# Row sums of 16,384 rows of 1,024: one row per partition moved from the blocks to the tail

## The chip, the cores and the metric

The kernel runs on one core of a Trainium2 chip. The metric is the device time of one execution in microseconds (us). Three runs of the kernel before took 160.62, 160.66 and 160.67 us; their median is 160.66.

## The reference

`x` has the shape 32 x 512 x 1024 in float32, so 16,384 rows of 1,024 numbers (4 KB each, 67.1 MB in all). Each row is summed, and the sum is multiplied by 0.5:

```python
def reference(x: np.ndarray, multiplier: float) -> np.ndarray:
    return (np.sum(x, axis=-1) * multiplier).astype(np.float32)
```

The result has 16,384 numbers, 64 KB.

## The kernel before

The rows are dealt out to the 128 partitions of the on-chip memory, 128 rows to each, in three groups (lines 39 to 50).

- The *blocks*: partition p owns `own` = 112 consecutive rows, rows 112p to 112p + 111 of the input. They are loaded in seven blocks of B = 16 rows per partition (64 KB per partition, 8 MB per block).
- The *tail*: after the 128 x 112 block rows come 128 x 15 rows, of which partition p owns `tail` = 15 consecutive ones. They are loaded last, in pieces of 7, 5 and 2 rows (`pieces`, line 157), and the 15th row in two cuts of 608 and 416 numbers into a tile of its own, `end` (lines 162 to 165).
- The *lead*: the last 128 rows of the input, one to a partition, loaded first (line 114).

So in the input a partition's block rows start 112 x 4 KB = 448 KB after those of the partition before, and its tail rows 15 x 4 KB = 60 KB after.

All DMAs are issued by SyncE (SP) on one queue, in the order of the program: the lead, blocks 0 to 6, the tail's five loads, and three stores. There are three buffers of 16 rows per partition, `buf`. Blocks 0, 1 and 2 find them free; their loads and the lead's are moved to the program's entry (lines 203 to 229) so that they start before anything else. The load of block b, from 3 on, waits until VectorE has summed block b - 3 (`freed`, line 122); the tail goes into block 4's buffer (line 156).

VectorE waits for each block and sums all its 16 rows with one `reduce_sum` (line 134), and scales the 16 sums into `res` with a small second instruction (line 140). Block 6, the last, is halved: VectorE takes 8 rows, and ScalarE takes the other 8, one instruction pair each (`act_row`, line 89, with the running sum written to a column of `res`). In the tail the rows are dealt by the set `on_act` (line 175): ScalarE takes rows 4, 5, 6, 10, 11 and 13, VectorE takes the others with `dve_sum` (line 98), which adds a row's two halves and sums them in one instruction. The 15th row is VectorE's: first the 608 numbers, then the 416 together with the first part's sum (lines 187 to 192).

Three stores follow on SP. The early store (line 167) writes the blocks' results, 112 numbers (448 B) per partition, and is issued when VectorE and ScalarE are done with block 6. The lead's store (line 171) writes 4 x 32 numbers. The last store (line 195) writes the tail's results, 15 numbers (60 B) per partition, and waits for both engines. The program ends when all three have landed.

Of the kernel before, what the change touches and what calls it, by code (L numbers as in the profile page):

```python
# [9 lines left out]
def kernel(  # L10
# [24 lines left out]
    rows = N // P  # L35
# [3 lines left out]
    B = 16  # L39
    n_blocks = rows // B  # L40
    assert N == P * rows and rows == n_blocks * B
    own = rows - B
    tail = B - 1
    lead0 = P * (own + tail)
    x_rows = x_flat[0 : P * own, :].rearrange("(p c) d -> p c d", p=P)
    x_last = x_flat[P * own : lead0, :].rearrange("(p c) d -> p c d", p=P)
# [27 lines left out]
    def marks(i, engine):  # L74

        s = dve_done if engine == "dve" else act_done
        i.then_inc(s, 1)
        counts[engine] += 1
        return counts[engine]

    def load(name, dst, src, free=None):
        landed = sem(name)
        i = nc.sync.dma_start(out=dst, in_=src)  # L83
        if free is not None:
            i.wait_op(dve_done, free, "sem-ge")
        i.then_inc(landed, 16)
        return landed

    def act_row(t, r, col):
        return nc.scalar.activation(  # L90
            out=t[:, r, :],
            in_=t[:, r, :],
            func=mybir.ActivationFunctionType.Copy,
            scale=mul,
            accum_out=res[:, col : col + 1],
        )

    def dve_sum(row, dst, scale):
        mid = row.shape[-1] // 2
        return nc.vector.tensor_tensor_reduce(  # L100
            out=row[:, 0:mid],
            in0=row[:, 0:mid],
            in1=row[:, mid:],
            scale=scale,
            scalar=0.0,
            op0=ADD,
            op1=ADD,
            accum_out=dst,
        )
# [3 lines left out]
    freed = []  # L113
    lead_landed = load("lead_landed", lead, x_lead)
    for b in range(n_blocks - 1):
        c0 = b * B
        t = buf[b % bufs]
        landed = load(
            f"landed{b}",
            t,  # L120
            x_rows[:, c0 : c0 + B, :],
            freed[b - bufs] if b >= bufs else None,
        )
        h = B if b < n_blocks - 2 else B // 2
        if b == 0:
            nc.vector.wait_ge(lead_landed, 16)
            nc.vector.wait_ge(dve_done, zeroed)
            summed = marks(dve_sum(lead, lead_sq[:, 0:1], mul), "dve")
            turned = nc.vector.transpose(out=lead_tr, in_=lead_sq)  # L129
            turned.wait_op(dve_done, summed, "sem-ge")  # L130
            marks(turned, "dve")
        nc.vector.wait_ge(landed, 16)
        done = marks(
            nc.vector.reduce_sum(  # L134
                out=sums[:, c0 : c0 + h], in_=t[:, 0:h, :], axis=mybir.AxisListType.X
            ),
            "dve",
        )
        freed.append(done)
        scaled = nc.vector.tensor_single_scalar(  # L140
            out=res[:, c0 : c0 + h],
            in_=sums[:, c0 : c0 + h],
            scalar=mul,
            op=mybir.AluOpType.mult,
        )
        scaled.wait_op(dve_done, done, "sem-ge")
        early_dve = marks(scaled, "dve")
        if h < B:
            nc.scalar.wait_ge(landed, 16)
            for r in range(h, B):  # L150
                i = act_row(t, r, c0 + r)
            early_act = marks(i, "act")

    c0 = (n_blocks - 1) * B
    t = buf[(n_blocks - 1) % bufs]
    nc.sync.wait_ge(dve_done, freed[n_blocks - 1 - bufs])
    pieces = [(0, 7), (7, 12), (12, 14)]
    landed = [
        load(f"landed_p{k}", t[:, lo:hi, :], x_last[:, lo:hi, :])
        for k, (lo, hi) in enumerate(pieces)  # L160
# [11 lines left out]
    lead_stored = sem("lead_stored")  # L172
    lead_store.then_inc(lead_stored, 16)

    on_act = {4, 5, 6, 10, 11, 13}
    for k, (lo, hi) in enumerate(pieces):
        on = [r for r in range(lo, hi) if r in on_act]
        nc.scalar.wait_ge(landed[k], 16)
# [86 lines left out]
```

## Time and profile before

| What | Value |
|---|---|
| Median of 3 runs | 160.66 us |
| The profiled execution | 160.62 us |
| Its span in the profile | 159.3 us |
| Read from the chip's memory (HBM), written to it | 67.11 MB, 0.07 MB |
| Mean rate over the span | 422 GB/s |
| VectorE (DVE) busy | 120.2 us, 75% |
| ScalarE (ACT) busy | 16.3 us, 10% |
| Share of the DMA queue's packets of 16 engines' span | 98.0% |

Times in the profile count from the span's start. DVE is VectorE, ACT is ScalarE, SPq is the sequencer of SyncE, which issues the DMAs. A name such as `sums<-xb` tells the tile written and the tile read, with buffer numbers left out; `L134` is line 134. A DMA is carried out by up to 16 DMA engines, and it has landed when all have counted up its semaphore; each load here gives every partition one packet, so each of the 16 engines has 8 of them.

### The profile page before, as it was taken

Reading aid. Unit: us, or ns where it says so; the run is one execution under the profiler, and the core shown is the slowest. Engines: PE = TensorE matmul, PEld = TensorE weight load, DVE = VectorE, ACT = ScalarE, POOL = GpSimd, SP = SyncE. Lnnn points to the kernel's source line nnn. Section 1 sums busy time; section 2 is a strip of 40 time slices with the busy share of each in tenths; the row PEclk is TensorE's granted clock in tenths of the full one; section 3 lists DMA queues with packets and bytes.
Section 4 is the critical chain, followed back from the end, with each engine's and each line's share of the span. In section 5 each row is a group of like instructions: output and inputs, shape, how many; then the busy total and the mean of one; then the engine's idle time right before and its main releaser. Section 6 shows DMA issues by size and latency. Waiting matters only on the chain.

```text
span 159.3 us, 128 instructions
## 1 busy us (share of the span) xinstructions
DVE 120.2 (75%) x39; ACT 16.3 (10%) x29; POOL 0.2 (0%) x4
## 2 busy tenths in 40 slices
DVE  2000029999499995999869997899959999599744
ACT  2000000000000000000000000000000000099844
POOL 0000000000000000000000000000000000000000
DMA  9969989899699699699699898996996996999994
GB/s 395 510 280 527 411 379 527 379 411 527 263 527 527 263 527 527 263 527 494 296 527 428 362 527 379 411 527 280 510 527 263 527 527 263 436 403 433 442 397 144
DMA packets 2168, 67.18 MB, mean 422 GB/s; under 512 B 504, under 2 KB 632, under 8 KB 888
## 3 DMA queue, kind: packets, MB, share of 16 engines
q1 hardware_dynamic: 2168, 67.18, 98.0%
HBM read 67.11 MB, written 0.07 MB: 422 GB/s over the span
## 4 chain that ended last, share of the span: by engine, by line
DMA 75%; DVE 22%; SPq 1%; issue 0%
DMA xb<-in_x_dram 52%; DMA end<-in_x_dram 24%; DVE sums L134 22%; SPq L83 1%; DVE end L100 1%; DVE res L140 0%; DVE res L100 0%
## 5 line engine op out<-in xcount | busy, mean ns | idle before, releaser
L134 DVE TENSOR_REDUCE sums<-xb 128x16 f32<-128x16384 f32 (+1 forms) x7 | 112.0, 16001 | 30.3 <-DMA xb<-in_x_dram 30.3
L90 ACT ACTIVATE xb<-xb 128x1024 f32<-128x1024 f32 x14 | 14.6, 1046 | 138.1 <-DMA xb<-in_x_dram 138.0
L100 DVE CUSTOM_DVE_ANT_0 xb<-xb 128x512 f32<-128x512 f32 x8 | 5.1, 689 | 3.9 <-DMA xb<-in_x_dram 3.9
L90 ACT ACTIVATION_READ_ACCUMULATOR xb<-xb 128x1 f32 x14 | 2.6, 188 | 0.0
L111 DVE MEMSET end<- 128x2 f32 x1 | 0.1, 60 | 2.9 <-PEq L26 2.9
L90 ACT ACT_TABLE_LOAD x1 | 1.3, 1283 | 2.9 <-PEq L26 2.9
L140 DVE TENSOR_SCALAR res<-sums 128x16 f32<-128x16 f32 (+1 forms) x7 | 1.2, 174 | 0.2
L100 DVE CUSTOM_DVE_ANT_0 end<-end 128x304 f32<-128x304 f32 (+1 forms) x2 | 0.9, 428 | 0.1
L100 DVE CUSTOM_DVE_ANT_0 lead<-lead 128x512 f32<-128x512 f32 x1 | 0.7, 693 | 0.2 <-DMA lead<-in_x_dram 0.2
L100 DVE DVE_READ_ACCUMULATOR2_ANT res<- 128x1 f32 x9 | 0.8, 83 | 0.0
L129 DVE STREAM_TRANSPOSE lead_tr<-lead_sq 128x32 f32<-128x32 f32 x1 | 0.2, 211 | 0.0
L246 POOL MEMSET const-bfloat16-1.0<- 128x1 bf16 x1 | 0.1, 101 | 0.0
L246 POOL MEMSET const-uint8-127<- 128x1 uint8 x1 | 0.1, 101 | 0.0
L246 POOL MEMSET const-float32-0.0<- 128x1 f32 x1 | 0.1, 98 | 0.2 <-issue 0.2
L246 POOL MEMSET const-float32-1.0<- 128x1 f32 x1 | 0.1, 98 | 0.0
L112 DVE MEMSET lead_sq<- 128x32 f32 x1 | 0.1, 85 | 0.0
L100 DVE DVE_READ_ACCUMULATOR2_ANT end<- 128x1 f32 x1 | 0.1, 84 | 0.0
L100 DVE DVE_READ_ACCUMULATOR2_ANT lead_sq<- 128x1 f32 x1 | 0.1, 83 | 0.0
## 6 DMA issues: line engine op xcount, KB each, us to landing
xb<-in_x_dram SPq DMA_DIRECT2D x1, 3584.0 KB, 29.9
xb<-in_x_dram SPq DMA_DIRECT2D x1, 2560.0 KB, 35.7
xb<-in_x_dram SPq DMA_DIRECT2D x1, 1024.0 KB, 37.7
lead<-in_x_dram SPq DMA_DIRECT2D x1, 512.0 KB, 3.2
end<-in_x_dram SPq DMA_DIRECT2D x1, 304.0 KB, 37.9
end<-in_x_dram SPq DMA_DIRECT2D x1, 208.0 KB, 38.0
xb<-in_x_dram SPq DMA_DIRECT2D x7, 40.8
out_dram<-res SPq DMA_DIRECT2D x1, 56.0 KB, 9.6
```

Source lines behind the costliest of these rows:

```text
L83: i = nc.sync.dma_start(out=dst, in_=src)
L90: return nc.scalar.activation(out=t[:, r, :], in_=t[:, r, :], func=mybir.ActivationFunctionType.Copy, scale=mul, accum_out=res[:, col : co ...
L100: return nc.vector.tensor_tensor_reduce(out=row[:, 0:mid], in0=row[:, 0:mid], in1=row[:, mid:], scale=scale, scalar=0.0, op0=ADD, op1=ADD, ...
L111: marks(nc.vector.memset(end[:, at - 2 : at], 0.0), "dve")
L112: zeroed = marks(nc.vector.memset(lead_sq, 0.0), "dve")
L129: turned = nc.vector.transpose(out=lead_tr, in_=lead_sq)
L134: nc.vector.reduce_sum(out=sums[:, c0 : c0 + h], in_=t[:, 0:h, :], axis=mybir.AxisListType.X),
L140: scaled = nc.vector.tensor_single_scalar(out=res[:, c0 : c0 + h], in_=sums[:, c0 : c0 + h], scalar=mul, op=mybir.AluOpType.mult,)
L246: nc = _bacc.Bacc("TRN2", target_bir_lowering=False, num_devices=1)
```

## The change

A partition owns 111 consecutive rows in the blocks, 16 in the tail and still one of the lead. Block 0 shrinks to 15 rows; blocks 1 to 6 keep 16, and start a row earlier. The tail's first piece grows from 7 to 8 rows; the pieces of 5 and 2 and the last row in two cuts keep their sizes, one row further on. Of the eight rows of the first piece ScalarE takes 4 to 7, one more than before, and VectorE 0 to 3 as before; from piece 1 on both have what they had. In the input the pitch from partition to partition becomes 444 KB in the blocks and 64 KB in the tail. In the output the early store writes 444 B per partition and the last one 64 B. In block 0, VectorE sums 15 rows.

```diff
-    own = rows - B
-    tail = B - 1
+    own = rows - B - 1
+    tail = B
     lead0 = P * (own + tail)
...
     for b in range(n_blocks - 1):
-        c0 = b * B
+        c0 = max(b * B - 1, 0)
+        n = (b + 1) * B - 1 - c0
         t = buf[b % bufs]
         landed = load(
             f"landed{b}",
-            t,
-            x_rows[:, c0 : c0 + B, :],
+            t[:, 0:n, :],
+            x_rows[:, c0 : c0 + n, :],
             freed[b - bufs] if b >= bufs else None,
         )
-        h = B if b < n_blocks - 2 else B // 2
+        h = n if b < n_blocks - 2 else n // 2
...
-        if h < B:
+        if h < n:
             nc.scalar.wait_ge(landed, 16)
-            for r in range(h, B):
+            for r in range(h, n):
                 i = act_row(t, r, c0 + r)
...
-    c0 = (n_blocks - 1) * B
+    c0 = own
     t = buf[(n_blocks - 1) % bufs]
     nc.sync.wait_ge(dve_done, freed[n_blocks - 1 - bufs])
-    pieces = [(0, 7), (7, 12), (12, 14)]
+    pieces = [(0, 8), (8, 13), (13, 15)]
...
-    on_act = {4, 5, 6, 10, 11, 13}
+    on_act = {4, 5, 6, 7, 11, 12, 14}
```

## The prediction

> **What bounds the kernel now.** I read the page's first parts, then the chain that ended last, then the timeline, and last the DMA issues. First the busy times and the 40 slices (4 us each):
>
> ```profile
> DVE 120.2 (75%) x39; ACT 16.3 (10%) x29; POOL 0.2 (0%) x4
> ...
> DVE  2000029999499995999869997899959999599744
> ACT  2000000000000000000000000000000000099844
> ...
> DMA  9969989899699699699699898996996996999994
> ...
> q1 hardware_dynamic: 2168, 67.18, 98.0%
> ```
>
> VectorE idles for a quarter of the span, ScalarE works only in the last sixth. The one DMA queue was occupied for 98% of 16 engines' span. I don't read its 6s as pauses, because the landings below keep one pace. Now the chain, from its middle on:
>
> ```profile
> 59.50 40.80 DMA xb<-in_x_dram
> ...
> 118.91 37.93 DMA end<-in_x_dram
> 156.84 0.02 issue
> 156.87 0.50 DVE end L100 x2
> 157.37 0.02 issue
> 157.39 0.38 DVE end L100
> 157.77 0.01 DVE res L100
> ```
>
> VectorE's 17.23 us steps appear in this chain because a load waits for a free buffer, but the loads ahead of it in the queue were still running then, so they are not what costs. What ends the kernel is the last piece landing at 157.37, one short reduction, and the last store. The timeline shows the pace of the stream and the room around it (start, duration, in brackets the idle time before):
>
> ```profile
> 22.81 17.22 DVE L134 TENSOR_REDUCE sums<-xb 128x16 f32<-128x16384 f32 x1 [18.62 <-DMA xb<-in_x_dram]
> ...
> 42.25 17.22 DVE L134 TENSOR_REDUCE sums<-xb 128x16 f32<-128x16384 f32 x1 [2.01 <-DMA xb<-in_x_dram]
> ...
> 139.02 8.69 DVE L134 TENSOR_REDUCE sums<-xb 128x8 f32<-128x8192 f32 x1 [1.93 <-DMA xb<-in_x_dram]
> ...
> 147.25 0.19 ACT L90 ACTIVATION_READ_ACCUMULATOR xb<-xb 128x1 f32 x1
> 147.52 1.06 ACT L90 ACTIVATE xb<-xb 128x1024 f32<-128x1024 f32 x1
> ...
> 150.56 0.19 ACT L90 ACTIVATION_READ_ACCUMULATOR xb<-xb 128x1 f32 x1
> 153.63 1.06 ACT L90 ACTIVATE xb<-xb 128x1024 f32<-128x1024 f32 x1 [2.88 <-DMA xb<-in_x_dram]
> ...
> 157.80 0.35 SPq L195 DMA_DIRECT2D out_dram<-res  x1
> ```
>
> Block 0 wakes VectorE at 22.81, block 6 at 139.02: six blocks in 116.21 us, 19.37 us a block, 1.21 us a row (of 128 x 4 KB), or 8,388,608 B / 19.37 us = 433 GB/s. VectorE needs 17.2 + 0.2 of each 19.37 us. So the bytes in the one queue set the time.
>
> **The change part by part.** The profiled execution took 160.62 us: a span of 159.3 and 1.3 around it. The median of the runs shown is 160.66, so I add 0.04 at the end.
>
> *The stream.* Block 0 loses a row (-1.21 us), the first tail piece gains one (+1.21). Bytes, DMAs and packets per engine stay (each load gives a partition one packet, before and after). Sum 0. Blocks 0 to 6 land 1.21 us earlier, block 0 at about 21.6, block 6 at 137.8; the last rows lie as far from the end as before. Piece 0 landed at 147.50 (its count in the trace), 8.48 us after block 6; with eight rows it takes 9.69, from 137.8, and still lands at 147.5, piece 1 at 153.6, the ends at 156.84 and 157.37.
>
> *VectorE.* A row of the block reduction costs (17.22 - 8.69) / 8 = 1.07 us, so the first becomes 16.15 us; it starts 1.21 and ends 2.28 us earlier. The others end 1.21 earlier. That is off the path: VectorE waits 1.9 us for each block anyway. In the tail it still sums four rows of piece 0, three of piece 1 and one of piece 2, so its work after each landing is the same. 0.
>
> *SP's queue.* Load 3 waits for block 0's reduction (40.0, now 37.8), with blocks 1 and 2 queued before it. The five tail loads wait for block 4's (117.55, now 116.3), with blocks 5 and 6 queued, some 21 us of stream. The early store waits behind them for VectorE and ScalarE; none of these waits lengthens. 0. Without that cover an issue (0.4 us) would show as a gap in the stream.
>
> *ScalarE.* It gets a fourth row of piece 0, 1.04 us between two starts. Its half of block 6 now ends near 146.2 instead of 147.44, piece 0 lands at 147.5, four rows end at 150.75 + 1.04 = 151.8, and piece 1 lands at 153.6. The idle time of 2.88 us becomes 1.84. 0; if this cover were gone, 1.04 us would move on to piece 1's rows, less the 0.31 us that ScalarE idles before its last row and the 0.49 us from the last row's end (157.28) to VectorE's (157.77): at most 0.24 us at the end, too little for a rival.
>
> *The two stores.* The DMA issues, KB each and us from issue to landing:
>
> ```profile
> out_dram<-res SPq DMA_DIRECT2D x1, 56.0 KB, 9.6
> ...
> out_dram<-res SPq DMA_DIRECT2D x1, 7.5 KB, 1.4
> ```
>
> The early store is issued at 148.0 and lands 9.6 us later, at 157.6: its packets stand behind the loads on every engine. It will be issued 1.2 us earlier, at about 146.8, and land at the same time, after some 10.8 us. Its 128 runs become 444 B instead of 448 B. The last store's runs grow from 60 to 64 B, and are now multiples of 64 B from each other. By the trace's packet records (no view prints them singly) a 60 B packet takes 10 ns, a 128 B one 13, a 448 B one 25, with 8 for each engine: the 4 B cost at most 8 x 3 ns = 0.02 us. What alignment could give is bounded by the 0.39 us between the last 60 B packet's end (158.85) and its last completion count (159.24). But the early store, whose 448 B runs are multiples of 64 B apart, needed 0.51 us for that step, so the nearest row shows no gain. I take 0, ends -0.39 and +0.02.
>
> *Addresses.* This is the one part that the trace can't price directly. In the blocks, a partition's data lies 448 KB from the next one's, now 444; in the tail 60 KB, now 64. So the tail takes the kind of pitch that the blocks had (a multiple of 64 KB), and the blocks the kind the tail had (an odd multiple of 4 KB). Both kinds run at full pace now: blocks 1.21 us a row, tail pieces 8.48 / 7 = 1.21 and 6.10 / 5 = 1.22. The one place with stalls is block 0: its 64 KB packets take 2.418 us when undisturbed, but the first took up to 2.81; added over block 0 an engine lost 0.24 us on average and 0.46 at most, and from block 1 on next to nothing. Bounds: -0.46 (all of block 0's stalls belong to the 448 KB pitch and go) and +1.4 (the tail's three whole pieces, 8 packets an engine each as in block 0, each lose its worst 0.46). I take 0, since both kinds of pitch have a full-rate row.
>
> The Trainium skill, page "DMA: Bandwidth & Descriptors", section "Latency and other measured facts", speaks against the tail's part: copies slow with a partition pitch of a large power of two (512 KiB 207 GB/s each way, 2 MiB 164, 4 MiB 103), and 4 KiB of padding restored the rate. 64 KB is below the pitches it lists, and no run here shows one; an estimate by its step from 207 to 164 would be 16 rows x 1.21 us x 207/164 - 19.4 = +5.1 us, or 165.8.
>
> Sum: -1.21 + 1.21 + 0 = 0 on 160.62; with 0.04 for the median, **160.66 us**.
>
> **The rivals.** 0.2% is 0.32 us, about what a measurement of this kernel can tell from no change.
>
> - *The tail stalls* (slower). The 16 engines stream side by side, and with 64 KB between partitions they start each tail piece on alike addresses, as in block 0 before. Nothing after the tail can absorb a delay: every 0.1 us goes to the end. For it: block 0, whose pitch is a multiple of 64 KB, is where stalls were. Against it: blocks 1 to 6 had the same pitch and next to none, so block 0's may be start-up. Price 0.24 (one piece, mean engine) to 1.4; middle about 0.7, so 161.4, and from 0.32 us on it decides. The page's rule above goes this way, further than any row here.
> - *Block 0's stalls go* (faster). The counts of an engine's landing were 0.40 us apart over block 0 and still 0.50 at the last piece: the slowest engine carries its early loss to the end. If 444 KB spreads the first reads, up to 0.46 goes: about 160.25. Against it: the lead, contiguous, also had slow first packets (0.58 against 0.16 us), so start-up alone may do it.
> - *The early store becomes the last to land.* Runs of 444 B share 64 B units with neighbours. It would have to land 1.6 us later, at 159.24 instead of 157.6, to count at all; 2.3 us later would give 161.3. Against it: the 60 B runs share units too and land in 1.4 us.
>
> **How the numbers follow.** Forecast 0.50 (160.4 to 160.95 by itself: small address effects either way); tail stalls 0.25; block 0's stalls gone 0.19; early store 0.06. So faster 0.19, same 0.50, slower 0.25 + 0.06 = 0.31. The range goes from 160.2 (most of the faster case) to 161.4 (the middle of the tail case); outside lie about a third of the tail case, a quarter of the faster one and half of the early store's: 0.08 + 0.05 + 0.03 = 0.16.
>
> **What would show it.** Right: the first 128x15 reduction starts near 21.6 for 16.15 us, the half block near 137.8, four ScalarE rows of piece 0 end near 151.8, and VectorE's last wait ends at 157.4 again; the early store takes about 10.8 us to land. Wrong: piece 0, 1 or 2 more than 8.48 + 1.21, 6.10 and 2.50 us after the load before it (tail stalls); the block reductions starting more than 1.21 us earlier (the start was the cost); or the last store's landing moving from 1.4 us.

## The result, and the profile after

The changed kernel takes 160.90 us (median of 22 runs, 160.72 to 161.11), the kernel before 160.62 (22 runs, 160.52 to 160.99). The ratio is 1.0016, with a 95% interval from 1.0009 to 1.0022: 0.28 us slower, by less than the 0.32 us that the prediction called a change, but clear of no change. The profiled execution took 160.93 us, 0.31 more than the one of before.

The timeline of the changed kernel, with the lines that answer to those shown of before:

```profile
21.66 16.15 DVE L135 TENSOR_REDUCE sums<-xb 128x15 f32<-128x15360 f32 x1 [17.49 <-DMA xb<-in_x_dram]
...
41.34 17.22 DVE L135 TENSOR_REDUCE sums<-xb 128x16 f32<-128x16384 f32 x1 [3.33 <-DMA xb<-in_x_dram]
...
60.70 17.22 DVE L135 TENSOR_REDUCE sums<-xb 128x16 f32<-128x16384 f32 x1 [1.93 <-DMA xb<-in_x_dram]
...
138.10 8.69 DVE L135 TENSOR_REDUCE sums<-xb 128x8 f32<-128x8192 f32 x1 [1.92 <-DMA xb<-in_x_dram]
...
153.93 1.06 ACT L90 ACTIVATE xb<-xb 128x1024 f32<-128x1024 f32 x1 [1.84 <-DMA xb<-in_x_dram]
...
158.15 0.34 SPq L196 DMA_DIRECT2D out_dram<-res  x1
```

Each start against the kernel before, with the 1.21 us of the moved row taken off, tells where the time was lost. (The lines of before stand in the prediction.) Block 0 starts VectorE at 21.66, 1.15 earlier, so 0.06 late. Block 1 does at 41.34, against 42.25: 0.91 earlier, 0.30 late. Block 6, at 138.10 against 139.02, is 0.29 late still. From the tail on nothing is shifted any more, and ScalarE's first row of piece 1 starts at 153.93 against 153.63, 0.30 late; the last store is issued at 158.15 against 157.80. So 0.24 of the loss arose while block 1 was loaded, and was carried through the remaining 117 us, in which the pace is the old one (60.70 to 138.10 is four blocks of 19.35 us).

The chain of the changed kernel ends like that of before, 0.34 us later:

```profile
117.98 39.22 DMA end<-in_x_dram
157.19 0.02 issue
157.22 0.49 DVE end L100 x2
157.71 0.02 issue
157.73 0.38 DVE end L100
158.11 0.01 DVE res L100
```

And the DMA issues show both output stores as worked out, the early one at 10.8 us and the last one at 1.4 us as before, now with 64 B runs:

```profile
out_dram<-res SPq DMA_DIRECT2D x1, 55.5 KB, 10.8
...
out_dram<-res SPq DMA_DIRECT2D x1, 8.0 KB, 1.4
```

What can make a stream late by 0.3 us and leave its pace as it was? A load has landed when the last of 16 DMA engines has counted. The times of the counts are in the trace (no view prints them). From the first data packet on, the mean of the last load's 16 counts was 156.08 us before and 156.10 after: in this pair of profiles the average engine is as fast as ever. But the last count lay 0.26 us behind that mean before, and 0.57 after. In block 1 the 15 earlier counts of the changed kernel lie within 0.49 us, and one engine comes 0.34 us after all of them. In block 6 it is still 0.34 us. The counts don't name their engine; that it is the same one throughout is inferred from this steady gap, and it fits that each engine has its own fixed share of 8 packets in every load. A second pair of profiles (below) has means of 156.06 and 156.17 and last counts 0.21 and 0.46 behind them: there 0.25 of the loss is the late engine's and 0.1 the mean's.

### The profile page after: what moved, and what is told of

The parts are those of the page before. It is cut to its first block, busy times and chain, and to the rows that moved or that the text cites. A ratio compares the mean times of both kernels' runs of the same rounds, so it can differ in the third digit from the quotient of the medians.

```text
span 159.6 us, 130 instructions
## 1 busy us (share of the span) xinstructions
DVE 119.2 (75%) x39; ACT 17.3 (11%) x31; POOL 0.2 (0%) x4
## 4 chain that ended last, share of the span: by engine, by line
DMA 75%; DVE 22%; SPq 1%; issue 0%
DMA xb<-in_x_dram 51%; DMA end<-in_x_dram 25%; DVE sums L135 22%; SPq L83 1%; DVE end L100 1%; DVE res L141 0%; DVE res L100 0%
## 5 line engine op out<-in xcount | busy, mean ns | idle before, releaser
L135 DVE TENSOR_REDUCE sums<-xb 128x16 f32<-128x16384 f32 (+2 forms) x7 | 110.9, 15848 | 30.4 <-DMA xb<-in_x_dram 30.4
L90 ACT ACTIVATE xb<-xb 128x1024 f32<-128x1024 f32 x15 | 15.7, 1045 | 137.4 <-DMA xb<-in_x_dram 137.4
L141 DVE TENSOR_SCALAR res<-sums 128x16 f32<-128x16 f32 (+2 forms) x7 | 1.2, 174 | 0.2
```

Of the source, the lines that this page charges most:

```text
L90: return nc.scalar.activation(out=t[:, r, :], in_=t[:, r, :], func=mybir.ActivationFunctionType.Copy, scale=mul, accum_out=res[:, col : co ...
L135: nc.vector.reduce_sum(out=sums[:, c0 : c0 + h], in_=t[:, 0:h, :], axis=mybir.AxisListType.X),
L141: scaled = nc.vector.tensor_single_scalar(out=res[:, c0 : c0 + h], in_=sums[:, c0 : c0 + h], scalar=mul, op=mybir.AluOpType.mult,)
```

## The experiments

All medians below are of 11 or 12 runs, compared with runs of the kernel before on the same chip; `b_block512` has 10, and the second executions of both kernels are single ones. Each of the four groups ran on a chip of its own. The kernel before took 160.60 or 160.61 us on all four, but the full loss at 444 KB was seen only in the first group (`a_tail60`) and the third; in the second and the fourth the changed kernel itself was not timed. Where the input's addresses are altered, the rows that are read are not all of them or some twice, and only the time is of interest.

### Which pitch: each put in or taken out alone

```diff
 # b_block444 (in before), a_block448 (in the changed kernel, 112 for 111)
-    x_rows = x_flat[0 : P * own, :].rearrange("(p c) d -> p c d", p=P)
+    x_rows = bass.AP(x_flat.tensor, 0, [[111 * D, P], [D, own], [1, D]])
 # b_tail64 (in before), a_tail60 (in the changed kernel, 15 for 16)
-    x_last = x_flat[P * own : lead0, :].rearrange("(p c) d -> p c d", p=P)
+    x_last = bass.AP(x_flat.tensor, P * own * D, [[16 * D, P], [D, tail], [1, D]])
```

> The kernel before, with the input pitch of the blocks alone changed from 448 to 444 KB (a partition still reads 112 rows per partition, so neighbours read one row twice and the rows behind are left out). Theory 1, the 444 KB pitch costs the changed kernel's time in the first blocks (its counts of landing are 0.13 us late in block 0 and 0.38 from block 1 on): about +0.28 us, 160.9. Theory 2, the tail's 64 KB pitch: 0, 160.6. Theory 3, the new sizes (15 rows in block 0, runs of 444 and 64 B in the output, loads that start at odd rows): 0, 160.6.

> The kernel before, with the tail's pitch alone changed from 60 to 64 KB (each partition's fifteen rows start 16 rows apart, so some rows are left out). Theory 1 (444 KB pitch): 0, 160.6. Theory 2 (64 KB pitch): +0.28 us, 160.9, with the 20 KB packets of piece 1 at up to 0.95 us as in the changed kernel, where they took 0.76 before. Theory 3 (sizes): 0.

> The changed kernel, with the blocks' pitch put back to 448 KB (111 of every 112 rows are read in the blocks; the tail stays where it was). Theory 1: back to 160.6. Theory 2 and theory 3: 160.9 as the changed kernel.

> The changed kernel, with the tail's pitch put back to 60 KB (neighbouring partitions read one row twice). Theory 2: back to 160.6. Theory 1 and theory 3: 160.9 as the changed kernel. If both pitches carry a part, this and the run with 448 KB each win back a part.

| Run | us | ratio to before (95%) |
|---|---|---|
| b_block444 | 160.69 | 1.0007 (0.9998 to 1.0016) |
| b_tail64 | 160.76 | 1.0015 (1.0006 to 1.0023) |
| a_block448 | 160.67 | 1.0007 (0.9998 to 1.0016) |
| a_tail60 | 160.90 | 1.0020 (1.0011 to 1.0029) |

In the changed kernel the tail's pitch is worth nothing (160.90 with either), and the blocks' pitch most of the loss (160.67 without it). But put into the kernel before, 444 KB gives 160.69, not 160.9: the pitch needs something else of the change beside it. No theory was right as it stood. The 64 KB tail does stall when it is alone in the kernel before (160.76). Its piece 0 started ScalarE 8.67 us after block 6 (139.08 to 147.75), against 8.50 (139.02 to 147.52):

```profile
139.08 1.06 ACT L90 ACTIVATE xb<-xb 128x1024 f32<-128x1024 f32 x1 [134.93 <-DMA xb<-in_x_dram]
...
147.75 1.06 ACT L90 ACTIVATE xb<-xb 128x1024 f32<-128x1024 f32 x1 [0.25 <-DMA xb<-in_x_dram]
```

The packet records show it: the 28 KB packets of piece 0 took up to 1.25 us, against 1.07 before, which cost an engine 0.18 us on average. Piece 1, where the expectation looked for the stalls, had next to none (0.80 at most). In the changed kernel some of piece 1's 20 KB packets stalled too, to 0.95 us from 0.76 before, but the last count of piece 1 came 6.11 us after that of piece 0, as before (6.10). The engine that was already last did not lose there.

### Sizes, order and starting rows

With both old pitches, only the sizes and stores of the change are left. The other three change what comes with the 444 KB pitch: the place of the short block, or the row at which blocks 1 to 6 start.

```diff
 # a_both_pitches: a_block448 and a_tail60 together
 # a_short_last, in the changed kernel
-        c0 = max(b * B - 1, 0)
-        n = (b + 1) * B - 1 - c0
+        c0 = b * B
+        n = min(B, own - c0)
...
-        h = n if b < n_blocks - 2 else n // 2
+        h = n if b < n_blocks - 2 else (n + 1) // 2
 # b_444_odd, in b_block444
-            x_rows[:, c0 : c0 + B, :],
+            x_rows[:, max(c0 - 1, 0) : max(c0 - 1, 0) + B, :],
 # a_skip, in the changed kernel, x_rows with own + 1 rows at the 111-row pitch
-            x_rows[:, c0 : c0 + n, :],
+            x_rows[:, b * B : b * B + n, :],
```

> The changed kernel with both pitches of before, 448 KB in the blocks and 60 KB in the tail; what is left of the change is the sizes (15 rows in block 0, 8 in piece 0, the two stores). If the late engine needs the 444 KB pitch: 160.6 to 160.7, the 16 counts of a block's landing about 0.5 us apart, as before. If the sizes or the stores cost by themselves: 160.9, counts 0.8 us apart from block 1 on as in the changed kernel.

> The changed kernel with the block of 15 rows moved from the first to the last place: blocks 0 to 5 have 16 rows, block 6 has 15, of which VectorE sums 8 and ScalarE 7. Pitches and stores are those of the changed kernel and the output is the reference's. Theory A (a short first block at 444 KB pitch lays one engine behind the others at the border of blocks 0 and 1) and theory B (loads that start at odd rows at 444 KB pitch do): counts 0.5 us apart, 160.65 to 160.75. If the tail's pitch, the stores or the split of the tail are the cause: 160.9.

> The kernel before with the 444 KB pitch in the blocks, full blocks of 16 rows, but blocks 1 to 6 read from one row earlier, so at the odd rows at which the changed kernel reads them (row 15 is read twice). Theory A (short first block): 160.65 to 160.75, as with the pitch alone, counts 0.5 us apart. Theory B (odd starts): 160.9, one engine 0.3 us behind from block 1 on.

> The changed kernel with its short first block, but blocks 1 to 6 read from one row later, so at the even rows at which the kernel before reads them (row 15 of each partition is left out, row 111 is the next partition's first). Theory A: 160.9, one engine 0.3 us behind from block 1 on. Theory B: 160.65 to 160.75, counts 0.5 us apart.

| Run | us | ratio to before (95%) |
|---|---|---|
| a_both_pitches | 160.73 | 1.0005 (0.9996 to 1.0014) |
| a_short_last | 160.70 | 1.0004 (0.9995 to 1.0013) |
| b_444_odd | 160.80 | 1.0009 (1.0000 to 1.0018) |
| a_skip | 160.76 | 1.0007 (0.9998 to 1.0016) |

The sizes and the stores alone gave 0.13 us by the medians; the interval goes from 0.06 us faster to 0.22 slower, so these runs can't tell it from nothing. `a_short_last` has the changed kernel's pitches, stores and tail, and 15 rows in block 6 instead of block 0; it computes everything and is not slower than before by a margin that can be told. `a_skip` keeps the short first block and reads blocks 1 to 6 from the next row; it took 160.76, about halfway between the two kernels by the medians, and its profile has no engine behind. That speaks for theory B, the starting rows, more than for A, but does not decide it. `b_444_odd` fits B only in part: 160.80, between the two expectations, and its profile has no single engine behind in block 1.

### Is it made in the first two blocks?

```diff
 # a_early448; a_late448 with 111 and 112 exchanged
-    x_rows = x_flat[0 : P * own, :].rearrange("(p c) d -> p c d", p=P)
+    x_rows = bass.AP(x_flat.tensor, 0, [[112 * D, P], [D, own], [1, D]])
+    x_rows_late = bass.AP(x_flat.tensor, 0, [[111 * D, P], [D, own], [1, D]])
...
-            x_rows[:, c0 : c0 + n, :],
+            (x_rows if b < 2 else x_rows_late)[:, c0 : c0 + n, :],
```

> The changed kernel with blocks 0 and 1 alone at the old pitch of 448 KB (some rows are left out, some read twice); blocks 2 to 6, the tail and the stores are those of the changed kernel. Theory E: what costs is one DMA engine that falls behind in blocks 0 and 1, and the pitch does nothing once the stream runs: about 160.72, as with all blocks at 448 KB, last count of the last load 0.25 us behind the mean of the 16. If each block at 444 KB adds its part: 5/7 of the loss stays, 160.85.

> The mirror image: blocks 0 and 1 as in the changed kernel, at 444 KB, blocks 2 to 6 at 448 KB. Theory E: 160.9 as the changed kernel, with one engine about 0.3 us behind from block 1 on. If each block adds its part: 160.77.

> The changed kernel once more, for a second profile. If the late engine belongs to the kernel: counts of block 1's landing 0.75 to 0.85 us apart, the last of them 0.3 us behind the one before. If it was the luck of one execution: 0.5 us apart.

> The kernel before once more, for a second profile. Counts of the landings 0.45 to 0.55 us apart from block 1 on, the last load's last count 0.26 us behind the mean of the 16 as in the first profile, if that is the kernel's and not the execution's.

`a_early448` took 160.66 us, ratio 1.0002 (0.9993 to 1.0010); `a_late448` took 160.91, ratio 1.0019 (1.0010 to 1.0029). Both are theory E. Five blocks out of seven at the new addresses cost nothing that can be told, and the first two alone cost everything. The second executions took 160.90 (changed) and 160.52 (before); the late engine was there again, by 0.25 us in block 1, a little less than expected. One line tells the kernels apart, the second reduction with the idle time before it; here from `a_early448`, then `a_late448`, then the second profile of the changed kernel:

```profile
41.13 17.22 DVE L136 TENSOR_REDUCE sums<-xb 128x16 f32<-128x16384 f32 x1 [2.99 <-DMA xb<-in_x_dram]
```

```profile
41.29 17.22 DVE L136 TENSOR_REDUCE sums<-xb 128x16 f32<-128x16384 f32 x1 [3.27 <-DMA xb<-in_x_dram]
```

```profile
41.34 17.22 DVE L135 TENSOR_REDUCE sums<-xb 128x16 f32<-128x16384 f32 x1 [3.24 <-DMA xb<-in_x_dram]
```

VectorE waits 3.0 or 3.1 us for block 1 where no engine falls behind in it, and 3.2 to 3.3 where one does. In `a_late448` the packet records show it: among all packets near the border of blocks 0 and 1 only two were over their 2.418 us by more than 0.015, by 0.21 and then 0.10, the second starting where the first ended. Losses in later blocks exist too, one profile each: in `a_early448` blocks 2 and 3 woke VectorE 19.46 us apart instead of 19.35, with 27 long packets in block 3.

### The place of the reads, or their distances?

```diff
 # a_shift, in the changed kernel: all blocks one row further on
+    x_rows = bass.AP(x_flat.tensor, D, [[111 * D, P], [D, own], [1, D]])
 # b_444_shift, in before: all blocks 15 rows further on
+    x_rows = bass.AP(x_flat.tensor, 15 * D, [[111 * D, P], [D, own], [1, D]])
 # b_block512, in before
+    x_rows = bass.AP(x_flat.tensor, 0, [[128 * D, P], [D, own], [1, D]])
```

> The changed kernel with all blocks read one row (4 KB) further on in the input: the same sizes and the same distances between all reads of the blocks, but blocks 1 to 6 start at multiples of 64 KB from the start of a partition's 444 KB as in the kernel before, and block 0 at one row. If the place of the reads within the input counts (theory B): 160.7, counts of block 1 0.5 us apart. If only their distances from each other count (a short first block at 444 KB): 160.9 and one engine 0.25 to 0.3 us behind.

> The kernel before with 444 KB pitch and full blocks, all of them read 15 rows further on, so that all seven start 60 KB behind a multiple of 64 KB within a partition's share, as blocks 1 to 6 of the changed kernel do. If the place counts (theory B): 160.85, with an engine behind. If the distances count: 160.7, as with the 444 KB pitch alone.

> The kernel before with the blocks' pitch at 512 KB, a power of two (112 of every 128 rows are read). It doubles the suspected cause: if 16 streams side by side at alike addresses stall each other, a power of two is the worst case and the blocks should land later than every 19.36 us, each block by some tenths: 161.5 or more. If the pitch counts only in the first microseconds, until the engines have drifted apart: 160.6 to 161. [...]

| Run | us | ratio to before (95%) |
|---|---|---|
| a_shift | 160.64 | 0.9999 (0.9990 to 1.0008) |
| b_444_shift | 160.73 | 1.0005 (0.9997 to 1.0014) |
| b_block512 | 160.92 | 1.0015 (1.0006 to 1.0024) |

`a_shift` has the changed kernel's sizes, pitches, stores and work, its block reads all 4 KB further on, and the loss is gone. Its block 1 and its end:

```profile
41.08 17.22 DVE L135 TENSOR_REDUCE sums<-xb 128x16 f32<-128x16384 f32 x1 [3.00 <-DMA xb<-in_x_dram]
...
157.84 0.34 SPq L196 DMA_DIRECT2D out_dram<-res  x1
```

So the distances between the block reads seem not to be enough to bring the loss about; where they lie in the input counts (or where they lie to the lead's and the tail's reads, which were not moved). One rival is untested: the changed kernel was not timed on this chip, so that the chip makes the difference is not ruled out, for `a_shift` as for `a_skip` and `a_short_last`.

`b_444_shift` doesn't confirm the simple rule behind theory B by its median: reads 60 KB behind a multiple of 64 KB in every block gave 160.73, nearer to the 160.69 of the pitch alone than to the 160.85 that B asked for. But its profile, of the slowest of its 11 executions (160.97), has the late engine that B asked for, 0.31 us behind all others, and from block 0 on, which starts VectorE 0.47 us later than before:

```profile
23.28 17.22 DVE L134 TENSOR_REDUCE sums<-xb 128x16 f32<-128x16384 f32 x1 [18.77 <-DMA xb<-in_x_dram]
```

So the loss can come and go between executions of one kernel. What stays open is which reads of which engines meet, and why there.

`b_block512` slows the start and not the stream, in its one profile, of an execution of 161.15 us:

```profile
23.47 17.22 DVE L134 TENSOR_REDUCE sums<-xb 128x16 f32<-128x16384 f32 x1 [18.98 <-DMA xb<-in_x_dram]
42.83 17.22 DVE L134 TENSOR_REDUCE sums<-xb 128x16 f32<-128x16384 f32 x1 [1.93 <-DMA xb<-in_x_dram]
...
139.57 8.69 DVE L134 TENSOR_REDUCE sums<-xb 128x8 f32<-128x8192 f32 x1 [1.92 <-DMA xb<-in_x_dram]
```

Block 0 lands 0.66 us later than before (23.47 against 22.81), and then six blocks take 116.10 us, against 116.21. Its 16 counts lie 0.99 us apart in block 0, against 0.40.

The spread of the 16 counts (first to last) and the last count's distance from their mean, in us, of every profile. The profiled execution is one of those behind the median and can lie apart from it, so both are given:

| Kernel | median | profiled | spread, block 0 | spread, block 1 | last load's last count behind the mean |
|---|---|---|---|---|---|
| before, twice | 160.62 | 160.62, 160.52 | 0.40, 0.45 | 0.49, 0.48 | 0.26, 0.21 |
| changed, twice | 160.90 | 160.93, 160.90 | 0.54, 0.42 | 0.83, 0.67 | 0.57, 0.46 |
| a_tail60 | 160.90 | 160.84 | 0.51 | 0.67 | 0.48 |
| a_late448 | 160.91 | 160.83 | 0.41 | 0.68 | 0.45 |
| a_early448 | 160.66 | 160.79 | 0.59 | 0.59 | 0.28 |
| a_block448 | 160.67 | 160.72 | 0.61 | 0.61 | 0.24 |
| a_both_pitches | 160.73 | 160.76 | 0.68 | 0.67 | 0.40 |
| a_short_last | 160.70 | 160.71 | 0.57 | 0.52 | 0.28 |
| a_skip | 160.76 | 160.76 | 0.46 | 0.51 | 0.27 |
| a_shift | 160.64 | 160.61 | 0.50 | 0.45 | 0.21 |
| b_block444 | 160.69 | 160.64 | 0.45 | 0.46 | 0.28 |
| b_tail64 | 160.76 | 160.84 | 0.43 | 0.43 | 0.39 |
| b_444_odd | 160.80 | 160.73 | 0.57 | 0.57 | 0.38 |
| b_444_shift | 160.73 | 160.97 | 0.80 | 0.77 | 0.48 |
| b_block512 | 160.92 | 161.15 | 0.99 | 0.97 | 0.53 |

In the changed kernel, `a_tail60` and `a_late448` alone, four profiles in all, does the spread grow by more than 0.1 us from block 0 to block 1. `a_both_pitches` starts with a wide spread and loses little, so a wide spread by itself does not set the time: the mean of the 16, between 156.05 and 156.32 us in these profiles, takes part in it.

## Why the prediction was wrong

**The step that failed** is the term "Addresses", taken as 0 "since both kinds of pitch have a full-rate row". The change measured +0.28 us (in its profile 0.30, of which 0.06 in block 0 and 0.24 in block 1), and 0.23 of it goes when the blocks get their old pitch back (`a_block448`); in the changed kernel the new addresses of blocks 0 and 1 alone are enough for all of it (`a_late448`). The rows I priced it by, 1.21 us a row in the blocks and in the tail, are rows of the stream once it runs. They say that the blocks' pitch costs nothing there, and 512 KB does not either; they say nothing of the first 40 us, in which one engine can fall 0.3 us behind the others. Nor did the full-rate row hold for the tail by itself, where `b_tail64` lost 0.17 us. Why these reads stall an engine stays open. I had seen block 0's stalls and the 0.50 us between first and last count, and used them only as a bound for a gain and for the tail. The bound on the other side, that the new addresses could add a second helping of the same stalls at the start, is missing in that step: about 0.46 us, the worst engine's loss in block 0, would have held the 0.3. A smaller slip in the same rows: the 8.48 us of piece 0 sets its landing count against VectorE's start on block 6; from count to count it is 8.51.

**The rivals.** Tail stalls: packets that stall at the 64 KB pitch with nothing behind to absorb it are shown in the tail of `b_tail64` (0.17 us, somewhat under the lowest price named, 0.24); that alike addresses are the reason is argued only. They are not what slowed the changed kernel, since `a_tail60` is no faster. Block 0's stalls go: wrong, the 444 KB pitch alone gave 160.69 and not 160.25. The early store: no, it landed after 10.8 us, as forecast, and the end came from the loads.

**What held.** The bytes sum to 0: the mean of the engines moved by 0.02 us in one pair of profiles and by 0.1 in the other. VectorE's first reduction took the 16.15 us forecast. ScalarE's four rows were hidden with 1.84 us of idle time left, the figure forecast. The last store took 1.4 us with 64 B as with 60 B runs. The time lies in the forecast's own 160.4 to 160.95, which allowed for small address effects either way, but that is luck: the sum has no term that would bring it there, and the runs tell 0.28 us from nothing where the prediction took 0.32 as the limit.

The estimate by the Trainium skill (page "DMA: Bandwidth & Descriptors", section "Latency and other measured facts"), 165.8 us, did not come about: the trace has piece 0 at 9.72 us for eight rows, 1.21 a row, at a 64 KB pitch. The same section of the Trainium skill gives 207 GB/s at a 512 KiB pitch against 214 as the full rate, for copies between tensors in HBM. The loads of `b_block512` show no such loss of 3% once the stream runs (19.35 us a block, as at 448 KB); that run was 0.3 us slower, and its profile has the loss in block 0.

No version here beat the kernel before; `a_shift`, which leaves a row out, ties with it.

## What to carry to other kernels

Where one DMA stream sets the time, ask for the slowest of its 16 engines and not for the mean rate: here a loss of some 0.3 us by one engine in the first blocks went to the end almost in full, each engine having its fixed share of every load. A change of addresses with as many bytes as before can make or take away such a loss, so price it by the first loads' stalls, in both directions, and not by the settled pace. In the profile it shows as one interval between two block landings that is too long by some tenths, with the later ones at the old pace.

## What the runs showed of the hardware that was not expected

Moving all block reads by 4 KB was worth 0.26 us (160.90 to 160.64, on different chips), with every instruction and every size the same. A pitch of 512 KB cost 0.66 us of landing time in block 0 of one profile and nothing per block after it. And the same 64 KB tail cost 0.15 us (median) in the kernel before and nothing in the changed kernel. That the last engine already ran apart from the others there is not the whole reason: in `a_shift` the engines stay together, the tail's pitch is 64 KB, and no packet of pieces 0 and 1 took longer than its 1.21 and 0.76 us.
